# A hybrid layer's input projection, by blocks of full products or by seven products of halves

## The chip, the core and the metric

The kernel runs on one core of a Trainium2 chip. The metric is the time on the device, in microseconds (us), of one launch. Engines are named as in the profile: PE (TensorE, with its weight loads PEld), DVE (VectorE), ACT (ScalarE), POOL (GpSimd) and SP (SyncE, which issues the DMAs here). A matmul result lies in PSUM, in banks of 512 float32 columns.

## The reference

One layer over 2048 tokens of 1024 features, in float32: a norm, one projection to 5120 columns, and two branches that are gated, merged and added to the input.

```python
h = rms_norm(x, norm_gain)
z = h @ w_in                                   # 1024 -> 5120
q, k, v, gate_a, u_s, gate_s, merge_logits = split(z)      # 512 each, the last 2048
q, k = rms_norm of each sub-head of 64, with gains
o_a = diff_attention(q, k, v, ...) * silu(gate_a)          # 4 heads x 2, block-causal
o_s = s5_branch(u_s, ...) * silu(gate_s)                   # diagonal state space, GELU, GLU
g_a, g_s = split(sigmoid(merge_logits + merge_gate_b))
x + (g_a * (o_a @ proj_attn) + g_s * (o_s @ proj_ssm)) @ w_out
```

The change is in the second line, and in when the state space's work is done beside it.

## The kernel before

Everything is held by feature: a tile has 128 features or columns on its partitions and a block of `TB` = 512 tokens along its row. A float32 product is made by `split3` from three matmuls: each operand is cut into an upper half (the cast to the matmul's own float32 type) and a lower half (the rest), and upper × upper, upper × lower and lower × upper are added in one bank. The function `hilo` makes the two halves, the cast on ACT and the difference on DVE or POOL.

`phase1` keeps all of x on chip as two halves, `hh` and `hl`, four blocks of 512 tokens each, not normed; the norm is a factor per token (`E`, later `R`) that is applied to the results. The weights come in 20 groups `g` of 256 columns; groups 0 and 1 are q, 2 and 3 k, 4 and 5 v, 8 and 9 u, the others the gates. Of each tile of 128 columns and each block of tokens, 8 × 3 matmuls of 512 columns fill one bank (`proj`, `proj1`); v is made with the tokens as the stationary operand, 24 matmuls of 256 columns for 128 tokens (`value`). Order: q and v of group 0, then q, v, k, k, u. After each block of q or k comes `qk_norm`: two squares, their sum, the sum over sub-heads on PE (`ms`, lines 231 and 232), a Newton step for the inverse root, and the product's two halves, stored to DRAM as Q or K (four stores of 256 KB).

Behind u stands `mid()`: `ssm_prep` (the state space's matrices for chunks of eight steps, with long complex products on POOL and DVE), `ssm_states` (the scan over chunks), `attn_consts`, and `ssm_out` (16 iterations, each of 12 matmuls of 256 columns into `ps_y`). Then `early()`, which loads K, V and Q of the first head, and the 24 tiles of the gates; the last two tiles (`LATE`) leave their last block of tokens to `last`, called beside the attention. Attention, `glu`, `proj_ssm` and `Tail` follow.

The code is written in this order, but a scheduler in the framework reorders instructions between engines by its own simulated times and fixes one order per engine; each engine then takes its instructions strictly in that order, and waits come only from data and buffers. A pool's tag is a ring of buffers: a new tile waits until the last user of the buffer's old tile, a store's landing included, is through.

Of the kernel before, what the change touches and what calls it, by code (L numbers as in the profile page):

```python
# [21 lines left out]
def f(ap):  # L22
    """The float32 view of a float32r operand."""
    return ap.bitcast(F32)
# [12 lines left out]
LATE = 2  # L37

def split3(nc, out, wh, wl, xh, xl, start, stop):
    """out += w.T x in float32: the three products of the halves that matter at 24 bits."""
    nc.tensor.matmul(out, wh, xh, start=start, stop=False)  # L44
    nc.tensor.matmul(out, wh, xl, start=False, stop=False)  # L45
    nc.tensor.matmul(out, wl, xh, start=False, stop=stop)  # L46
# [43 lines left out]
def newton(nc, k, pool, t, w, out, c=1.0, tags=("n", "n"), bufs=2):  # L90
    """out = c * t ** -0.5 over [128, w]: exp(-ln/2) and one Newton step."""
# [9 lines left out]
def phase1(tc, k, I, mid, early, keep):  # L101
    """The projections of the normed input, and steps that the last of them wait for: the gates' last columns
    over the last tokens."""
    nc = tc.nc
    with ExitStack() as es:
        def pool(name, bufs, e=es, **kw):
            kw = kw or {"side": "right"}
            return e.enter_context(tc.tile_pool(name=name, bufs=bufs, reuse_waits="tile", **kw))

        rp, k.wp = pool("rp", 1, keep), pool("wp", 1, keep)  # L110
        pm = pool("pm", 5, space=PSUM)
        hh, hl = [None] * NTB, [None] * NTB
        for t in reversed(range(NTB)):
            hp = pool(f"hp{t}", 1, keep if t == NTB - 1 else es)
            hh[t] = hp.tile([128, 8, TB], F32R, name=f"hh{t}")
            hl[t] = hp.tile([128, 8, TB], F32R, name=f"hl{t}")
        E = rp.tile([128, T], F32, name="E")
        rc = k.cp.tile([128, 16], F32, name="rc")

        BUFS = {"x": 4, "s": 3, "q": 2, "t": 2, "n": 2, "o": 2, "v": 2}  # L120
        W = {}

        def et(tag, name, dtype=F32):
            return k.ep.tile([128, TB], dtype, tag=tag, name=name, bufs=BUFS[tag])

        def load_w(g, eng=None):
            """Steps that load 256 columns in quarters and split them."""
            W[g] = []
            for i in range(4):
                if i % 2 == 0:  # L130
                    wh = k.wp.tile([128, 4, 256], F32R, tag="wh", bufs=4, name="wh")
                    wl = k.wp.tile([128, 4, 256], F32R, tag="wl", bufs=4, name="wl")
                    W[g].append((wh, wl))
                raw = k.wp.tile([128, 2, 256], F32, tag="wraw", bufs=2, name="wraw")
                o = slice(2 * (i % 2), 2 * (i % 2) + 2)
                nc.sync.dma_start(raw, I["win"][g][:, 2 * i:2 * i + 2])
                if eng:
                    eng.tensor_copy(wh[:, o], raw)  # L138
                else:
                    nc.scalar.copy(wh[:, o], raw)  # L140
                (eng or nc.gpsimd).tensor_tensor(out=wl[:, o], in0=raw, in1=f(wh[:, o]), op=ALU.subtract)  # L141
                yield

        def load_w1(c):
            """One tile of 128 columns in halves, split."""
            wh, wl = (k.wp.tile([128, 8, 128], F32R, tag="wl", bufs=4, name="w1") for _ in range(2))
            for i in range(2):
                raw = k.wp.tile([128, 4, 128], F32, tag="wraw", bufs=2, name="wraw")
                o = slice(4 * i, 4 * i + 4)
                nc.sync.dma_start(raw, I["win"][c // 2][:, o, 128 * (c % 2):128 * (c % 2) + 128])  # L150
                nc.scalar.copy(wh[:, o], raw)
                nc.vector.tensor_tensor(out=wl[:, o], in0=raw, in1=f(wh[:, o]), op=ALU.subtract)
            return wh, wl

        def wk(g, kk, cs):
            return [w[:, kk % 4, cs] for w in W[g][kk // 4]]

        def load_x(t):
            """Steps that load a block of x in halves, and its norms."""
            acc = et("t", "acc")  # L160
            xs = {}
            lag = 2

            def square(kk):
                sq = acc if kk == 0 else et("q", "sq")
                nc.scalar.activation(out=sq, in_=xs[kk], func=AF.Square)
                if kk:
                    nc.gpsimd.tensor_tensor(out=acc, in0=acc, in1=sq, op=ALU.add)

            for kk in range(8):  # L170
                xs[kk] = et("x", "xs")
                nc.sync.dma_start(xs[kk], I["xT"][kk * 128:(kk + 1) * 128, t * TB:(t + 1) * TB])
# [201 lines left out]
NH = 4  # L374
# [836 lines left out]
```

## Time and profile before

| what | value |
|---|---|
| median of three runs | 1813.46 us (1805.32 to 1816.14) |
| span of the profiled execution | 1807.6 us |
| the profiled execution's own time | known by its span alone, 5.9 us below the median |
| mean granted PE clock | 0.979 |
| busy share: PE, PEld, DVE, ACT, POOL | 94%, 79%, 55%, 38%, 18% |
| DMA | 239.06 MB, mean 132 GB/s |

A busy time counts an instruction from start to end; matmuls overlap, so the price of one more is the distance between two starts, which is shorter than its own duration. Rows of the view by lines give, after the bar, the busy sum in us, the mean of one in ns, and the idle time ahead of the group with what ended it. Rows of the view of waits give the engine, tile and line that waited, what it waited for, the sum in us, how often, and the longest. A row of the chain gives the start, the length and the work that the end hung on.

### The profile page before, as it was taken

What the parts mean: (1) busy time and instruction counts of PE and PEld (TensorE: products, weight loads), DVE (VectorE), ACT (ScalarE), POOL (GpSimd) and SP (SyncE); (2) the same over time, 40 slices, a digit from 0 to 9 for tenths busy, and PEclk for the clock granted to TensorE, in tenths of its full rate; (3) what the DMA queues carried; (4) which work ended last, traced back from release to release, by engine and by line L of the source; (5) the groups of instructions that cost most, each with busy time, mean ns of one, the idle gap of its engine ahead of it and who ended that gap; (6) DMA issues with size and microseconds to landing.
All of it is one profiled execution on the core that took longest, in us unless ns stands there. A gap on an engine that the chain in (4) does not pass through costs nothing.

```text
span 1807.6 us, 24838 instructions
## 1 busy us (share of the span) xinstructions
PE 1701.5 (94%) x8720; PEld 1432.4 (79%) x8720; DVE 997.1 (55%) x2400; ACT 682.3 (38%) x1404; POOL 328.1 (18%) x442
## 2 busy tenths in 40 slices
PE   7879798889699999999999999999999999999999
PEld 5777786677588887887888878878888879888887
DVE  7644314469832495495223277678677678643331
ACT  5443222220123413311344366667554567511100
POOL 4331110004200000000345334553011022100000
PEclk9989899999899999999999999999999999999999
DMA  5332322233444323225656584763554543554532
GB/s 168 102 100 87 92 73 72 69 105 84 126 139 121 122 76 122 80 71 158 185 153 169 171 262 116 198 212 112 193 178 133 161 139 117 186 156 151 148 100 82
DMA packets 213005, 239.06 MB, mean 132 GB/s; under 512 B 41456, under 2 KB 151440, under 8 KB 211856
## 3 DMA queue, kind: packets, MB, share of 16 engines
q1 hardware_dynamic: 212880, 237.47, 43.5%
q8 instruction: 69, 1.13, 0.3%
q14 instruction: 56, 0.46, 0.1%
HBM read 146.44 MB, written 90.96 MB: 131 GB/s over the span
## 4 chain that ended last, share of the span: by engine, by line
PE 58%; DMA 17%; DVE 16%; ACT 3%; issue 3%; POOL 1%; SPq 1%; DVEq 0%; ACTq 0%; POOLq 0%
PE ps_p L44 8%; PE ps_p L45 8%; PE ps_p L46 8%; DMA K<-ql 5%; PE ps_o L568 5%; DVE t L879 4%; DMA Q<-ql 4%; PE ps_o L45 3%; PE ps_o L46 3%; PE ps_o L44 3%; PE ps_s L528 3%; PE ps_s L529 3%; PE ps_t L560 2%; DVE V L879 2%; PE ps_a L46 2%
## 5 line engine op out<-in xcount | busy, mean ns | idle before, releaser
L44 PE MATMUL ps_p<-hh,w 128*128 128x512 f32 x896 | 353.6, 395 | 2.4 <-DVE u L313 1.2
L45 PE MATMUL ps_p<-hl,w 128*128 128x512 f32 x896 | 353.2, 394 | 0.0
L46 PE MATMUL ps_p<-hh,w 128*128 128x512 f32 x896 | 352.7, 394 | 0.0
L44 PEld LDWEIGHTS ps_p<-hh,w 128*128 128x128 f32 x896 | 170.5, 190 | 38.0 <-DVE q L240 2.0
L46 PEld LDWEIGHTS ps_p<-hh,w 128*128 128x128 f32 x896 | 170.4, 190 | 35.3 <-issue 0.7
L45 PEld LDWEIGHTS ps_p<-hl,w 128*128 128x128 f32 x896 | 170.4, 190 | 34.5 <-issue 0.7
L541 ACT ACTIVATE e<-e,mm 128x640 f32<-128x640 f32 (+11 forms) x96 | 136.2, 1419 | 63.8 <-DVE mm L539 62.9
L568 PE MATMUL ps_o<-V,at 128*128 128x128 f32 x1088 | 148.5, 276 | 2.3 <-ACT sq L574 1.8
L568 PEld LDWEIGHTS ps_o<-V,at 128*128 128x128 f32 x1088 | 141.4, 192 | 9.3 <-ACT sq L574 2.3
L329 DVE TENSOR_TENSOR z<-ps_p,E 128x512 f32<-128x512 f32 x96 | 65.9, 686 | 132.7 <-PE ps_p L46 132.7
L531 DVE TENSOR_SCALAR_CACHE_REDUCE e<-ps_s 128x512 f32<-128x512 f32 (+1 forms) x192 | 120.6, 640 | 31.2 <-PE ps_s L529 29.7
L528 PE MATMUL ps_s<-K,Q 128*128 128x512 f32 (+3 forms) x320 | 129.0, 405 | 1.1 <-DVE e L531 0.8
L529 PE MATMUL ps_s<-K,Q 128*128 128x512 f32 (+3 forms) x320 | 115.9, 365 | 0.0
L44 PE MATMUL ps_qk<-hh,wh 128*128 128x512 f32 x256 | 101.6, 403 | 12.6 <-DVE wh L138 7.7
L45 PE MATMUL ps_qk<-hl,wh 128*128 128x512 f32 x256 | 101.2, 399 | 1.4 <-DVE hl L175 1.4
L46 PE MATMUL ps_qk<-hh,wl 128*128 128x512 f32 x256 | 101.9, 398 | 0.3 <-DVE wl L141 0.3
L335 ACT ACTIVATE z<-z,hmb 128x512 f32<-128x512 f32 x64 | 46.3, 723 | 144.6 <-DVE z L329 131.0
L560 PE MATMUL ps_t<-ident,e 128*128 128x128 f32 x544 | 85.1, 274 | 4.6 <-ACT at L562 2.5
L551 DVE SCALAR_TENSOR_TENSOR e<-e,cf 128x128 f32<-128x128 f32 (+7 forms) x64 | 88.2, 1378 | 1.4
L562 ACT COPY at<-ps_t 128x512 f32<-128x512 f32 (+3 forms) x160 | 79.3, 522 | 18.4 <-PE ps_t L560 17.8
L560 PEld LDWEIGHTS ps_t<-ident,e 128*128 128x128 f32 x544 | 66.4, 141 | 16.6 <-ACT at L562 4.2
L534 DVE CUSTOM_DVE_ANT_0 e<-ps_s,nb 128x384 f32<-128x384 f32 (+3 forms) x128 | 70.1, 552 | 16.6 <-PE ps_s L529 15.5
(334 smaller groups left out, 3464.4 us busy)
## 6 DMA issues: line engine op xcount, KB each, us to landing
wraw<-win SPq DMA_DIRECT2D x80, 256.0 KB
TM<-z SPq DMA_DIRECT2D x30, 512.0 KB
t<-TM SPq DMA_DIRECT2D x40, 256.0 KB
xs<-xT SPq DMA_DIRECT2D x32, 256.0 KB
u<-US SPq DMA_DIRECT2D x64, 128.0 KB
K<-K SPq DMA_DIRECT2D x8, 1024.0 KB
Q<-Q SPq DMA_DIRECT2D x32, 256.0 KB
Q<-Q SPq DMA_DIRECT2D x64, 128.0 KB
```

Source lines behind the costliest of these rows:

```text
L44: nc.tensor.matmul(out, wh, xh, start=start, stop=False)
L45: nc.tensor.matmul(out, wh, xl, start=False, stop=False)
L46: nc.tensor.matmul(out, wl, xh, start=False, stop=stop)
L528: nc.tensor.matmul(ps, Q[:, 0, s, 128 * b:128 * b + 128], Kt[s][:, ks], start=True, stop=False)
L529: nc.tensor.matmul(ps, Q[:, 1, s, 128 * b:128 * b + 128], Kt[s][:, ks], start=False, stop=True)
L531: nc.vector.tensor_scalar(out=et[:, ks], in0=ps, scalar1=0.0, scalar2=3e38, op0=ALU.add, op1=ALU.min, accum_out=mc[:, i:i + 1])
L541: nc.scalar.activation(out=et, in_=et, func=AF.Exp, bias=mm, scale=-1.0, accum_out=su)
L551: nc.vector.scalar_tensor_tensor(out=e[0], in0=e[1], scalar=cf, in1=e[0], op0=ALU.mult, op1=ALU.add)
L560: nc.tensor.transpose(pt[:, x], e[:, o:o + 128], k.ident)
L562: nc.scalar.copy(AT[g][:, :w], pt[:, :w])
L568: nc.tensor.matmul(po, AT[x // 4][:, x % 4], Vt[x // 8][:, x % 8], start=x == 0, stop=x == n - 1)
L879: tt = lambda o, a, b, op: eng.tensor_tensor(out=o, in0=a, in1=b, op=op)
```

## The change

The projection is done with Strassen's scheme in Winograd's form: features and tokens are cut in two halves each (and the columns of a group in two tiles of 128), and seven products of half size take the place of eight. It runs over one half of 1024 tokens at a time (`sb`), and per half over all 20 groups.

- `first` loads two blocks of tokens, norms them, and makes seven blocks (`BLOCKS`) of 4 × 128 features by 512 tokens: three quarters of the normed x and four sums of quarters. Each is split into halves in a ring of seven buffers, and also stored in DRAM (`BD`).
- `second` does the same for the other two blocks of tokens, in steps between the groups of the first half, into DRAM only. Its norms are products on POOL; x is read twice.
- `turn` loads the other half's seven blocks (28 DMAs of 256 KB) and splits them (ACT and DVE). It is called before the second half, and again between the gates, since the gates run over the second half first.
- `weights` loads four quarters of a group, makes four sums on POOL and splits seven tiles (ACT and DVE). All 20 groups are thus loaded, summed and split twice, once per half.
- `product` is 12 matmuls of 512 columns; `group` makes seven of them, 84 matmuls, with three banks X, Y and Z; ACT copies banks out in the middle of their accumulation, and three of the four results are finished by a sum (two on DVE from PSUM, one on POOL).
- q and k, v, u and the gates are then handled from SBUF. v is turned by four transposes per tile (64 in all) rather than made in its own layout. `qk_norm` takes all its eight tiles from one ring "q" of six; its sum of squares and lower halves of q and k are on POOL.
- The preparation of the state space is a generator, stepped between the groups of the second half, with smaller tiles (complex products of 288 elements a row on POOL, eight by seven, where they had 576). `ssm_out` has a lasting pool `so`, whose tiles `Tail` uses later. `early` comes only after all gates, and nothing is left for beside the attention.

```diff
+BLOCKS = ("11", "21", "T2", "T1", "T3", "22", "T4")
+    def halves(self, n, j, src):
+        nc, b = self.nc, self.B[n]
+        nc.scalar.copy(b[:, 0, j], src)
+        nc.vector.tensor_tensor(out=b[:, 1, j], in0=src, in1=f(b[:, 0, j]), op=ALU.subtract)
+    def norm(self, x, kk, R, eng):
+        gc = self.k.gain[:, kk:kk + 1]
+        if eng is self.nc.vector:
+            eng.scalar_tensor_tensor(out=x, in0=x, scalar=gc, in1=R, op0=ALU.mult, op1=ALU.mult)
+        else:
+            self.nc.scalar.activation(out=x, in_=x, func=AF.Copy, scale=gc)
+            eng.tensor_tensor(out=x, in0=x, in1=R, op=ALU.mult)
+    def combine(self, x11, x12, x21, x22, eng):
+        tt = lambda o, a, b: eng.tensor_tensor(out=o, in0=a, in1=b, op=ALU.subtract)
+        tt(x11, x12, x11)
+        tt(x12, x22, x12)
+        tt(x22, x22, x11)
+        tt(x21, x21, x22)
+        return {"T1": x11, "T3": x12, "T4": x21, "T2": x22}
...
+    def turn(self, sb, tile):
+        for n in BLOCKS:
+            self.slot(n)
+            for j in range(4):
+                x = tile()
+                self.nc.sync.dma_start(x, self.BD[sb][n][j])
+                self.halves(n, j, x)
+    def weights(self, g):
...
+        yield split(a[0, 0])
+        yield split(a[0, 1])
+        s1 = raw()
+        tt(s1, a[1, 0], a[1, 1], ALU.add)
+        tt(a[1, 0], a[0, 0], a[1, 0], ALU.subtract)
+        tt(a[0, 0], s1, a[0, 0], ALU.subtract)
...
+    def product(self, ps, w, n, first):
+        b = self.B[n]
+        for j in range(4):
+            split3(self.nc, ps, w[:, 0, j], w[:, 1, j], b[:, 0, j], b[:, 1, j], first and j == 0, j == 3, not first)
+    def group(self, g, put):
...
+        X = self.bank("ps_x")
+        self.product(X, next(w), "11", True)
+        m1 = copy(X, "m1")
+        Z = self.bank("ps_z")
+        self.product(Z, next(w), "21", True)
+        put(0, 0, Z, m1)
+        self.product(X, next(w), "T2", False)
+        u2 = copy(X, "u2")
+        Y = self.bank("ps_y")
+        self.product(Y, next(w), "T1", True)
+        m5 = copy(Y, "m5")
+        self.product(X, next(w), "T3", False)
+        u3 = copy(X, "u3")
+        put(1, 1, u3, m5)
+        self.product(Y, next(w), "22", False)
+        put(0, 1, Y, u2)
+        self.product(X, next(w), "T4", False)
+        put(1, 0, X, None)
...
+                    for a in range(2):
+                        p.u(8 + a, sb)
+                        step()
+                        p.qk(a, sb, k.qg, k.QT[a])
+                        step()
+                    for a in range(2):
+                        p.v(4 + a, sb)
+                        step()
+                        p.qk(2 + a, sb, k.kg, k.KT[a])
+                        step()
...
+        mid()
+        for g in gates:
+            p.gate(g, 1)
+        p.turn(0, lambda: tr.tile([128, TB], F32, tag="tr", bufs=4, name="x"))
+        for g in gates:
+            p.gate(g, 0)
+    early()
```

First piece: PE at the end of the gates. Before, the attention's first scores (`ps_s`) stand among the matmuls of the gates' last tile (`ps_p`):

```order
L44 MATMUL ps_p<-hh_138,w_8417 128x512
L45 MATMUL ps_p<-hl_139,w_8417 128x512
L46 MATMUL ps_p<-hh_138,w_8418 128x512
L528 MATMUL ps_s<-K,Q 128x128 x2
L528 MATMUL ps_s<-K,Q 128x256
L529 MATMUL ps_s<-K,Q 128x128 x2
L529 MATMUL ps_s<-K,Q 128x256
L44 MATMUL ps_p<-hh_133,w_8322 128x512
```

Now, on the same engine, the last of the gates (`ps_x<-B,w`) is followed by four iterations of the state-space output (rows 642 to 688, twelve matmuls each, of which the first few and the last are shown) before the first scores:

```order
641 L40 MATMUL ps_x<-B,w 128x512 x2
642 L40 MATMUL ps_y<-u,th 128x256
643 L40 MATMUL ps_y<-uh,tm 128x256
644 L40 MATMUL ps_y<-xh,wh 128x256
688 L40 MATMUL ps_y<-xh,w 128x256
689 L653 MATMUL ps_s<-K,Q 128x128 x2
690 L653 MATMUL ps_s<-K,Q 128x256
```

What moved: the output of the state space, which lay wholly under the gates, partly ends behind them, and the first scores come behind it.

Second piece: PE between the two norms of the first group of q in the first half. `ms` is a norm's sum over sub-heads; `ps_x`, `ps_y`, `ps_z` are the banks of the groups that follow:

```order
L386 MATMUL ms<-sh,bones 128x512
L40 MATMUL ps_x<-B,w 128x512 x5
L387 MATMUL ms<-sl,bones 128x512
L40 MATMUL ps_x<-B,w 128x512 x24
L40 MATMUL ps_y<-B,w 128x512 x12
L40 MATMUL ps_z<-B,w 128x512 x10
L40 MATMUL ps_x<-B,w 128x512 x12
L40 MATMUL ps_z<-B,w 128x512 x2
L40 MATMUL ps_x<-B,w 128x512 x12
L386 MATMUL ms<-sh,bones 128x512
```

Before, one `ms` came per block of tokens, a block's 24 × 2 matmuls behind the last; now both norms of a group come due at its end, and their two `ms` stand inside the groups behind it, 77 matmuls apart.

Third piece: POOL in the second half. Before, it had the preparation's complex products (`bigc`, 576 elements) in one run with nothing else between:

```order
L693 TENSOR_TENSOR bigc_3572<-bc,P_3488 128x576
L693 TENSOR_TENSOR bigc_3571<-bc,P_3489 128x576
L693 TENSOR_TENSOR cp_3573<-bigc_3572,bigc_3571 128x576
L693 TENSOR_TENSOR bigc_3571<-bc,P_3488 128x576
L693 TENSOR_TENSOR bigc_3572<-bc,P_3489 128x576
```

Now they (`big`, 288 elements) stand between weight sums (L267), the third result's sum (L323), sums of squares (L382) and lower halves of q and k (L984):

```order
L267 TENSOR_TENSOR raw<-raw 128x512
L984 TENSOR_TENSOR ql<-sq,qh 128x512
L818 TENSOR_TENSOR big_2959<-bC,P_2934 128x288
L818 TENSOR_TENSOR big_2960<-bC,P_2933 128x288
L984 TENSOR_TENSOR ql<-sq,qh 128x512
L267 TENSOR_TENSOR raw<-raw 128x512
L323 TENSOR_TENSOR z<-u_2826,m_2809 128x512
L818 TENSOR_TENSOR cp_3574<-big_2960,big_2959 128x288
L382 TENSOR_TENSOR sq<-sq 128x512
```

What moved: work of the norms, the weights and the state space that lay on other engines or in other stretches shares one queue.

More of the change, by code (lines that the diff above doesn't have):

```diff
@@ L35, with split3 @@
 TAIL = [3, 0, 1, 2]
[L37 to L46, printed above, removed]
+def split3(nc, out, wh, wl, xh, xl, start, stop, more=False):
+    mm = lambda w, x, a, b: nc.tensor.matmul(out, w, x, start=a, stop=b, skip_group_check=more)
+    mm(wh, xh, start, False)
+    mm(wh, xl, False, False)
+    mm(wl, xh, False, stop)
 def consts(tc, k, I):
@@ L104, in phase1 @@
+def phase1(tc, k, I, prep, mid, early):
     nc = tc.nc
     with ExitStack() as es:
[L106 to L153, printed above, removed]
@@ L340, in phase1 @@
-        cols = (12, 13, 14, 15, 20, 21, 22, 23, *range(24, 40))
-        n = len(cols) - LATE
-        for c in cols[:n]:
-            gate(c, range(NTB))
-        w = {c: gate(c, range(NTB - 1)) for c in cols[n:]}
-    def last(ps):
-        for c in (*cols[-2:], *cols[n:-2]):
-            gate(c, (NTB - 1,), w[c] if c in cols[-2:] else None, ps)
-    return last
+        p = Proj(tc, k, I, es)
+        gates = (6, 7, 10, 11, *range(12, 20))
+        with ExitStack() as e1:
+            p.pn = p.pool("pn", e1, space=PSUM)
+            nc.sync.dma_start(k.ident, I["ident"])
+            with ExitStack() as e0:
+                p.ep, p.ex, p.nx = p.pool("ep0", e0), p.pool("ex0", e0), 16
+                p.first()
+            p.ep = p.pool("ep", e1)
+            for sb in range(2):
+                with ExitStack() as e2:
+                    if sb == 0:
+                        p.ex, p.nx = p.pool("ex", e2), 5
+                        it = p.second()
+                    else:
+                        it = prep()
+                    step = lambda: next(it, None)
+                    for a in range(2):
[8 more added lines that the diff above has]
+                        step()
+                    for _ in it:
+                        pass
+                    if sb == 0:
+                        p.turn(1, p.x)
@@ L756, in ssm_prep @@
         bb = [t(f"bb{i}", [128, 16, 16]) for i in range(2)]
-        big = [t(f"big{i}", [128, 4 * 144]) for i in range(2)]
+        big = [t(f"big{i}", [128, 288]) for i in range(2)]
+        yield
         b16 = [b[:, :256].rearrange("p (a b) -> p a b", b=16) for b in big]
@@ new lines, in ssm_matrices @@
+        for q in range(0, 16, 2):
+            out = [p.tile([128, 2, 8, 16], F32, tag=f"cp{i}", name=f"wn{i}") for i in range(2)]
+            s = slice(q, q + 2)
+            cmul(v, out[0], out[1], cc[0][:, s], cc[1][:, s], pj[0][:, s, 0:8], pj[1][:, s, 0:8], w[0], w[1])
+            ps = k.pF.tile([128, 2, 2, 2, 64], F32, tag="F", bufs=k.NF, name="ps_w")
+            for y in range(2):
+                for r in range(2):
+                    nc.tensor.transpose(ps[:, y, r].rearrange("p x q -> p (x q)"),
+                                        out[r][:, y].rearrange("p j h -> p (j h)"), k.ident)
+            wi = p.tile([128, 2, 2, 2, 64], F32, tag="wi", name="wi")
+            for y in range(2):
+                nc.scalar.copy(wi[:, y].rearrange("p x r q -> p r x q"), ps[:, y])
+            nc.sync.dma_start(k.WD[:, 2 * q:2 * q + 4], wi.rearrange("p y x r q -> p (y x) (r q)"))
+            if q == 6:
+                yield
@@ L817, in ssm_prep @@
+    yield
     with ExitStack() as e2:
-        with tc.tile_pool(name="sp4", bufs=1, side="right", reuse_waits="tile") as p2:
+        with tc.tile_pool(name="sp4", bufs=1, reuse_waits="tile") as p2:
             dd = p2.tile([16, 32], F32, name="dd")
```

569 lines of the change are left out of this document (307 added, 262 removed).

## The prediction

> **What bounds the kernel now.** I read the head of the page first, for the engine that is busy and the clock, and then a table of busy time by stage: up to 46 us the start, to 495 us q, k, v, u and the preparation of the state space, to 1046 us the gates with the scan and the state-space output beside them, then the attention and the rest.
>
> ```profile
> span 1807.6 us, 24838 instructions
> PE 1701.5 (94%) x8720; PEld 1432.4 (79%) x8720; DVE 997.1 (55%) x2400; ACT 682.3 (38%) x1404; POOL 328.1 (18%) x442
> ```
> ```profile
> 0.00:46.00 46.00, 33.33 (x170) 27.01 (x171) 32.95 (x53) 25.48 (x45) 19.52 (x25) 1.00 0.57 170
> 46.00:495.00 449.00, 381.43 (x1888) 322.19 (x1887) 234.49 (x543) 122.09 (x225) 81.99 (x63) 0.93 0.32 91
> 495.00:1046.00 551.00, 545.59 (x2552) 453.16 (x2551) 259.43 (x595) 178.22 (x343) 77.05 (x87) 0.99 0.44 133
> 1046.00:1808.00 762.00, 741.16 (x4114) 630.03 (x4112) 470.19 (x1211) 356.49 (x792) 149.52 (x268) 1.00 0.50 154
> ```
>
> The columns are start and end, length, busy us of PE, its weight loads, VectorE, ScalarE and GpSimd, the granted clock, the DMA share and GB/s. PE is busy 545.59 of 551 us in the gates: fewer matmuls there are time saved. From 46 to 495 us it idles for 67.6 us (449 − 381.4) and its 381 us ran at 0.93 of the clock, another 381.4 × 0.07 = 27 us. What it waits for there stands in the waits and in the chain that ended last:
>
> ```profile
> PE ms L231 <- ACT sh L842: 39.0, 9, 11.0
> DVE ql L844 <- DMA Q<-ql: 64.5, 9, 9.5
> DVE ql L844 <- DMA K<-ql: 60.6, 12, 7.7
> ```
> ```profile
> 146.32 8.69 DMA Q<-ql
> ```
>
> The norms of q and k wait for their stores to land (8.69 us in this link), and PE waits for the norms. So one half of the projection is bound by PE, the other by side work.
>
> **The change: what PE saves.** Matmuls are pipelined, so their price is the step from start to start:
>
> ```profile
> 1029.69 0.39 PE L46 MATMUL ps_p<-hh,w 128*128 128x512 f32 x1
> ...
> 1046.01 0.40 PE L46 MATMUL ps_p<-hh,w 128*128 128x512 f32 x1
> 1046.24 0.50 PE L528 MATMUL ps_s<-K,Q 128*128 128x128 f32 x3
> ```
> ```profile
> 26.11 0.28 PE L252 MATMUL ps_v<-wh,hh 128*128 128x256 f32 x1
> ...
> 27.05 0.28 PE L253 MATMUL ps_v<-wl,hh 128*128 128x256 f32 x1
> ```
> ```profile
> 1181.40 1.79 PE ps_o L568 x16
> ```
>
> From the first to the third row lie 73 matmuls, so 512 columns cost 16.32/72 = 0.2267 us up to the last of them; 256 columns cost 0.94/8 = 0.1175, 128 columns 1.79/16 = 0.112. Before, the projection has 3456 matmuls of 512 columns (q and k 768, u 384, gates 2304) and 768 of 256 for v: 783.5 + 90.2 = 873.7 us. After, it has 20 groups × 2 halves × 84 = 3360 of 512 and 64 transposes: 761.7 + 7.2 = 768.9. PE saves **105 us**; a group costs 84 × 0.2267 = 19.04 us. The 48 matmuls left beside the attention (48 × 0.2267 = 10.9 us) go from there.
>
> **What the side engines gain.** The seven products are paid for in sums and splits on VectorE, GpSimd and ScalarE. How two of these share the memory shows at 46 us:
>
> ```profile
> 45.96 2.99 POOL L168 TENSOR_TENSOR acc<-acc,sq 128x512 f32<-128x512 f32 x2 [0.44 <-ACT sq L166]
> ...
> 45.99 1.81 DVE L96 TENSOR_TENSOR nw_a<-nw_y,tt 128x512 f32<-128x512 f32 x1
> ...
> 47.73 1.77 DVE L175 SCALAR_TENSOR_TENSOR hl<-xs,small,hh 128x512 fp32r<-128x512 f32 x1
> ...
> 49.42 0.68 DVE L97 SCALAR_TENSOR_TENSOR nw_a<-nw_a,nw_y 128x512 f32<-128x512 f32 x1
> ```
> ```profile
> 427.55 1.43 POOL L693 TENSOR_TENSOR cp<-bigc,bigc 128x576 f32<-128x576 f32 x1
> ...
> 427.64 1.37 DVE L693 TENSOR_TENSOR L<-big,big 128x16 f32<-128x16 f32 x1
> ```
> ```profile
> 902.76 0.69 DVE L946 TENSOR_TENSOR z<-ps_y,y 128x512 f32<-128x512 f32 x1 [0.26 <-POOL y L945]
> 902.81 1.30 POOL L844 TENSOR_TENSOR x<-x,xh 128x512 fp32r<-128x512 f32 x1
> ```
>
> A VectorE instruction with two inputs from SBUF takes 0.68 us alone and 1.81 or 1.77 beside a GpSimd one; even 16 elements a row last 1.37. One with an input from PSUM isn't held (0.69 beside 1.30). So the two engines take turns, and a pair costs about 1.79 us (the mean of 1.81 and 1.77); I split it as 0.57 for VectorE and 1.22 for GpSimd, estimates that leave out the latency at an instruction's start.
>
> The Trainium skill, page "SBUF — State Buffer", section "SBUF: two separate sides", says that GpSimd and a VectorE instruction with two SBUF inputs hold a shared pair of ports in turn for a whole instruction, and names no PSUM input among the blocked. The trace agrees (1.81 against 0.68; 0.69 beside 1.30). Had the two sums per group that read PSUM to wait too, as they don't by that rule, 40 groups would add 2 × 0.69 × 40 = 55 us to what follows.
>
> Counted from the code, VectorE with two SBUF inputs and GpSimd, both of 512 elements a row:
> - Start, first half and turn: 62 on VectorE for `first` (12 norms, 16 combinations, 28 splits, 6 in the inverse), 56 weight splits, 48 in eight norms, 24 in `second`, 28 in `turn`: 218 × 0.57 = 124 us. GpSimd: 4 + 32 weight sums + 8 + 24 in the norms + 30 in `second` = 98 × 1.22 = 120 us. From 12 us on (an estimate for the first loads and squares), taking turns ends at **256 us**.
> - Second half's eight groups and three gate groups: 125 × 0.57 = 71, 79 × 1.22 = 96. The preparation: 56 GpSimd instructions of 288 elements, about 0.7 us each by half of the row of 576 below, 39; VectorE some 40 (an estimate: a bit under half of the 83 us that it was busy in the two rows below). Sum 246, so 19 groups are done at **502 us**.
>
> ```profile
> L693 POOL TENSOR_TENSOR bigc<-bc,P 128x576 f32<-128x576 f32 x16 | 19.7, 1251 | 168.2 <-DVE P L693 167.7
> L168 POOL TENSOR_TENSOR acc<-acc,sq 128x512 f32<-128x512 f32 x28 | 39.3, 1404 | 62.6 <-ACT sq L166 61.6
> L152 DVE TENSOR_TENSOR w<-wraw,w 128x512 fp32r<-128x512 f32 x56 | 38.7, 714 | 0.1
> L151 ACT CAST w<-wraw 128x512 fp32r<-128x512 f32 x56 | 32.1, 618 | 93.4 <-PE ps_p L45 62.2 <-DMA wraw<-win 31.0
> ```
> ```profile
> 405.00:450.00 45.00, 44.73 (x198) 36.72 (x196) 43.48 (x147) 2.29 (x4) 20.67 (x18) 1.00 0.37 90
> 450.00:495.00 45.00, 30.09 (x120) 24.11 (x121) 39.49 (x164) 6.91 (x14) 13.47 (x11) 0.89 0.44 127
> ```
>
> PE alone would have them at 40 + 19 × 19.04 + 20 for norms and transposes = 422 us. Between 422 and 502 lies the main unknown; I take 502, since the trace shows the turn-taking wherever both engines have work.
>
> The other 21 groups are gates: 21 × 19.04 = 400 us of PE against 7 × 0.57 + 5 × 1.22 + 2 × 0.69 = 11.5 us a group on the side, so PE sets the pace, as from 495 to 1046 us. Added: 30 us of the state space's own matmuls (ps_k 64 × 0.112, the states 96 × 0.1175, half of ps_y 96 × 0.1175), and 25 where the scan's VectorE work or the second `turn` (28 splits at 0.714 = 20 us, ScalarE 28 × 0.618 = 17, in a group of 19) exceeds PE's. 502 + 455 = 957. Then four iterations of the state-space output stand alone on PE (the first piece in the section on the change): per iteration GpSimd alone has 4.7 us (tm, u, w, x and y at 0.74, 1.3, 0.74, 1.3 and 0.62), so 19 to 40, I take 26: the attention starts at **983** against 1046. That is a gain of 63.
>
> From there 762 − 10.9 (the late matmuls) + 5.6 (four iterations' 48 × 0.1175) + 12 = 769 us; the 12 are for K, V and Q of the first head, loaded only now, where before they lay under gates (an estimate between nothing and two landings of 8.69). The span is 983 + 769 = 1752, with 10 for waits in order that no sum holds **1762**. The profiled execution's time is known by its span of 1807.6, 5.9 below the median of the three runs, 1813.46; the same step gives 1768, and I say **1765**.
>
> Extra transfers: the first 256 us move about 51 MB (x 12.6, blocks stored 14.7 and loaded 7.3, weights 8.4, results 8.4), 200 GB/s, where 170 GB/s took a share of 0.57 (first row of the stages). At 0.67 this costs nothing by itself, unless landings grow.
>
> **The rivals.**
> - *The buffers hide the side work* and PE is paced by itself: 19 groups at 422 to 450 us, so 1690 to 1715. For it: half of GpSimd's work in the first half (`second`) may run late into the second. Against: the sums are of whole stages, and no buffer hides a mean. Chance 0.2.
> - *Copies in mid-accumulation come late.* Bank X is copied by ScalarE between its products, with 12 matmuls = 2.72 us to do so (one other product lies between). ScalarE has some 15 of 19 us of work per group in program order, splits of 0.618 us and norms among it. A copy late by 0.3 us, 160 times: 48 us, 1813, no change. Chance 0.12.
> - *Each wait costs clock too.* From 46 to 495 us the clock was 0.93 with 15% idle; 19.04/0.93 = 20.5 us is still under the 25 us a group that the turns take, so I cost it at nothing. If the waits come in one piece per group and PE then is at half pace over a critical stretch of about 1.7 us, 19 groups give 32 us: 1797. Chance 0.08. The Trainium skill, page "TensorE: Matmul & The Clock Gate", Part 1, has such a fall to half after an idle window of about 3.4 us; by it the loss per wait is an estimated 1.7 us, while the trace shows only the means.
> - *Stores set the pace, slower than before.* Place: `qk_norm`, ring "q" of six tiles with eight used per norm; the second norm of each q or k group can't have its sh before the first norm's qh has landed. Between the two `ms` PE has 77 matmuls (the second piece in the section on the change), 17.5 us; the chain between takes some 8.5 us (an estimate) and a landing. Up to a landing of 9 us it fits (8.69 above), beyond it PE stands for the rest, in eight groups. The gain of 48 is gone from a landing of 15 us; at 20, eight times 11, 88 us: 1853. For it: before, this was the chain's longest run of links. Against: those 17.5 us. Chance 0.17.
>
> **How the numbers follow.** My forecast, turn-taking to 502 us, has 0.43: 1735 to 1795. A measurement here tells about 1% from no change: faster is below 1795, slower above 1831. Faster: 0.43 + 0.2 and half of the clock's rival, 0.67; same: 0.12 + 0.04 and 0.02 of the stores' rival, its mild end, 0.18; slower: the rest of it, 0.15. The range leaves out most of the stores' rival and the tip of the first: **1690 to 1835**.
>
> **What would show it.** VectorE's splits (`w<-raw`) and combinations with means over 1.2 us and GpSimd busy over half of the first 500 us; PE idle by 70 to 100 us there, over 98% busy in the gates; the first ps_s of the attention near 983 us. If PE is busy throughout before 500 us, the first rival holds; waits of the banks for `copy` show the second; PE's `ms` waiting over 5 us eight times, with landings over 12, the fourth. I am wrong most likely in how far the turns overlap with PE across groups.

## The result, and the profile after

The changed kernel takes 1962.13 us (median; 1958.98 to 1967.9), the kernel before 1810.43 beside it: a ratio of **1.0849** (95% interval 1.0814 to 1.0884), slower by 152 us where a gain of 48 was forecast, and far outside the range. The head of the page and the table by stage, cut at the points that the prediction speaks of (columns as before):

```profile
span 1966.1 us, 24659 instructions
## 1 busy us (share of the span) xinstructions
PE 1683.8 (86%) x7948; PEld 1365.0 (69%) x7948; DVE 1253.2 (64%) x2438; ACT 917.0 (47%) x1816; POOL 701.2 (36%) x704
```
```profile
0.00:80.00 80.00, 42.50 (x115) 25.79 (x116) 61.20 (x83) 41.88 (x73) 23.30 (x26) 0.79 0.56 193
80.00:322.00 242.00, 164.82 (x641) 126.41 (x639) 130.05 (x137) 101.92 (x179) 125.66 (x85) 0.84 0.43 133
322.00:651.00 329.00, 261.80 (x1039) 199.51 (x1039) 219.56 (x380) 144.43 (x257) 171.74 (x139) 0.87 0.45 133
651.00:1165.00 514.00, 461.99 (x1998) 371.98 (x1997) 361.66 (x615) 252.75 (x474) 191.90 (x151) 0.94 0.44 143
1196.00:1966.00 770.00, 741.18 (x4112) 632.04 (x4112) 475.91 (x1218) 365.24 (x814) 173.22 (x288) 0.99 0.51 156
```

No engine is near its limit in the first three rows: PE idles in the projection, and DVE and POOL do too: up to 651 us at least one of the two is busy for 516 us, and for 135 us both stand. In the gates, where PE was busy 545.59 of 551 us, it now idles for 52 of 514. The starts of every 84th product matmul in the trace give the groups' times (group 0 is the first; in each half u and q alternate twice, then v and k, and from group 16 on all are gates):

| point | forecast, us | measured, us |
|---|---|---|
| group 8 begins (first half and turn done) | 256 | 322.6 |
| group 19 begins | 502 | 651.0 |
| last matmul of the gates | 957 | 1165.0 |
| first scores of the attention | 983 | 1196.1 |
| from there to the end | 769 | 770 |

Cutting each step from one matmul's start to the next into its price (0.2267 us per 512 columns), a gap (what is over, where it is more than 1.3 prices) and slow pace (the rest) gives PE's account up to the first scores: before, 908 us of price, 92 of gaps, 38 of slow pace; after, 815, **296** and 79. The change saved 93 us of matmuls and paid 204 in gaps and 41 in slow pace, 245 together.

### The profile page after: what moved, and what is told of

It reads as the page before. It is cut to its first block, busy times and chain, and to the rows that moved or that the text cites. A ratio compares the mean times of both kernels' runs of the same rounds, so it can differ in the third digit from the quotient of the medians.

```text
span 1966.1 us, 24659 instructions
## 1 busy us (share of the span) xinstructions
PE 1683.8 (86%) x7948; PEld 1365.0 (69%) x7948; DVE 1253.2 (64%) x2438; ACT 917.0 (47%) x1816; POOL 701.2 (36%) x704
## 4 chain that ended last, share of the span: by engine, by line
PE 33%; DVE 13%; DMA 13%; issue 5%; ACT 4%; POOL 3%; SPq 1%; POOLq 0%; ACTq 0%; DVEq 0%
PE ps_o L40 8%; PE ps_x L40 5%; DVE t L1019 4%; PE ps_a L40 3%; PE ps_p L40 3%; PE ps_o L693 3%; PE ps_y L40 3%; DVE w L264 2%; DVE V L1019 2%; PE ps_s L654 1%; PE ps_s L653 1%; PE ps_z L40 1%; PE ps_t L685 1%; DMA XD<-V 1%; DMA raw<-proj_attn 1%
## 5 line engine op out<-in xcount | busy, mean ns | idle before, releaser
L40 PE MATMUL ps_x<-B,w 128*128 128x512 f32 x1920 | 515.3, 419 | 109.4 <-ACT B L144 51.0
L40 PEld LDWEIGHTS ps_x<-B,w 128*128 128x128 f32 x1920 | 383.2, 203 | 213.8 <-ACT B L144 54.9
L267 POOL TENSOR_TENSOR raw<-raw 128x512 f32<-128x512 f32 x160 | 236.7, 1479 | 421.7 <-DMA raw<-win 209.8
L264 DVE TENSOR_TENSOR w<-raw,w 128x512 fp32r<-128x512 f32 x280 | 252.9, 908 | 164.8 <-ACT w L263 156.4
L40 PE MATMUL ps_y<-B,w 128*128 128x512 f32 x960 | 258.6, 412 | 24.3 <-ACT B L144 7.3
L40 PEld LDWEIGHTS ps_y<-B,w 128*128 128x128 f32 x960 | 188.8, 199 | 73.1 <-ACT B L144 9.0
L263 ACT CAST w<-raw 128x512 fp32r<-128x512 f32 x280 | 171.4, 622 | 81.4 <-POOL raw L267 41.2
L40 PE MATMUL ps_z<-B,w 128*128 128x512 f32 x480 | 123.5, 398 | 4.5 <-ACT B L144 4.5
L40 PEld LDWEIGHTS ps_z<-B,w 128*128 128x128 f32 x480 | 91.0, 192 | 24.7 <-ACT B L144 5.4
L40 PE MATMUL ps_o<-mm,wo 128*128 128x512 f32 x390 | 96.7, 394 | 0.1
```

The costliest lines, as they stand in the source:

```text
L40: mm = lambda w, x, a, b: nc.tensor.matmul(out, w, x, start=a, stop=b, skip_group_check=more)
L263: nc.scalar.copy(w[:, 0], src)
L264: nc.vector.tensor_tensor(out=w[:, 1], in0=src, in1=f(w[:, 0]), op=ALU.subtract)
L267: tt = lambda o, x, y, op: nc.gpsimd.tensor_tensor(out=o, in0=x, in1=y, op=op)
```

## The experiments

Ratios are against the kernel before, measured beside each version; "gain" is against the 1962 us of the changed kernel, "scores" the start of the attention (1196 in it). Differences of some 6 us tell nothing: prep_apart, whose engines work in the order of the changed kernel, differs from it by as much.

### The turns of DVE and POOL

Rows of the groups, the changed kernel first, then the one with all elementwise work of the projection on DVE:

```profile
L267 POOL TENSOR_TENSOR raw<-raw 128x512 f32<-128x512 f32 x160 | 236.7, 1479 | 421.7 <-DMA raw<-win 209.8 <-DVE w L264 81.9 <-issue 23.9
L264 DVE TENSOR_TENSOR w<-raw,w 128x512 fp32r<-128x512 f32 x280 | 252.9, 908 | 164.8 <-ACT w L263 156.4 <-POOL big L818 5.8 <-PE ps_y L40 1.2
```
```profile
L264 DVE TENSOR_TENSOR w<-raw,w 128x512 fp32r<-128x512 f32 x280 | 194.9, 701 | 45.3 <-ACT w L263 43.0 <-PE ps_v L40 2.0 <-issue 0.2
L267 DVE TENSOR_TENSOR raw<-raw 128x512 f32<-128x512 f32 x160 | 112.7, 705 | 62.2 <-DMA raw<-win 60.2 <-DVE w L264 0.9
```

A split took 0.908 us in the mean of all 280, against 0.701: the turns are there, at a fifth of what a full turn at every split would cost. In the changed kernel's trace 127 of the splits overlap an instruction of POOL and take 1.18 us in the mean, up to 1.81; the other 153 take 0.685. Half of POOL's idle time ahead of the sums (209.8 of 421.7 us) ends with the weights' load.

**weights_dve**, the four weight sums on DVE:

```diff
-        tt = lambda o, x, y, op: nc.gpsimd.tensor_tensor(out=o, in0=x, in1=y, op=op)
+        tt = lambda o, x, y, op: nc.vector.tensor_tensor(out=o, in0=x, in1=y, op=op)
```


> The four sums of each group's weights (160 in all) move from POOL to DVE; nothing is left out. Theory of turns (DVE with two SBUF inputs and POOL hold the memory in turn, and the amount of their work sets the first 19 groups): each sum costs 0.57 instead of 1.22 us, 50 us in the first 19 groups and little in the gates, about 1910 us. Theory of the late weight (PE waits for a link of the way from a weight's load over its sum and its split to the matmul, whatever the amount of work): four sums in a row get 3 us shorter, in the gates too, some 2 us in each of 40 groups, about 1880 us.

1919.98 us (1.0586, 1.053 to 1.0642), gain 42, scores at 1129.9: less than either theory, and nearer to the turns' 1910 than to the late weight's 1880.

**no_wsums**, no sums, and **sums_aside**, the same four sums into a scratch tile (both `raw` with `bufs=5`). Of sums_aside the first sum is shown; no_wsums has `s1 = a[1, 1]` and none of the four:

```diff
-        s1 = raw()
-        tt(s1, a[1, 0], a[1, 1], ALU.add)
+        s1, scr = a[1, 1], wp.tile([128, 4, 128], F32, tag="scr", bufs=1, name="scr")
+        tt(scr, a[1, 0], a[1, 1], ALU.add)
...
```


> The four sums of each group's weights are left out (three of the seven products use a plain quarter), the ring of loaded quarters is five tiles for four in use. Turns: 160 x 1.22 us of POOL's work gone, 93 us of it in the first 19 groups, little in the gates: about 1870 us. Late weight: a load goes straight to its split, so the gates come to 19 to 21 us a group instead of 25 and the first groups lose some 4 us each: about 1780 us.

> POOL makes the same four sums of each group's weights, from the same tiles, but into a scratch tile that nobody reads; the products use plain quarters as in the kernel without the sums, with the same ring. POOL's work, and its turns with DVE, stay; that the splits wait for the sums is gone. Turns: as the changed kernel, about 1960 us. Late weight: within 30 us of the kernel without the sums, below 1830 us.

1899.73 us (1.0474, 1.0426 to 1.0523) and 1977.94 us (1.0906, 1.0858 to 1.0954). With the sums made but needed by nobody nothing is gained; without them 62 us are. So it is not that the splits wait for the sums; POOL's work itself costs. Whether by its turns or by holding the loaded quarters, these two runs do not separate. The late weight falls in this form.

**all_dve**, norms, third sums, squares and lower halves on DVE as well (`nc.gpsimd` to `nc.vector` at L164, L218, L323, L382 and the `ql` of `qk_norm`):

> All of the projection's elementwise work on POOL (weight sums, third sums, sums of squares, norms, lower halves of q and k) moves to DVE; POOL keeps the state space's. Nothing is left out. Turns: 177 instructions in the first 19 groups cost 0.57 instead of 1.22 us, 115 us less, and 40 to 50 us less in the rest: about 1810 us. Late weight: as with the weight sums on DVE or a little more, 1850 to 1880 us, since DVE's queue gets longer ahead of every split.

1913.37 us (1.055, 1.0508 to 1.0591), scores at 1108.4: POOL is idle from 80 us to the end of the first half, so there are no turns, and 49 us are gained, not 150. Groups 1 to 6 still take 25.9 us in the mean (28.0 in the changed kernel). Taking POOL's work away thus recovers a third of the loss. It is not a clean price of the turns, since DVE does that work instead.

**no_wsums6**, as no_wsums with `bufs=6`:

> As the kernel without weight sums (1900 us), but the ring of loaded quarters has six tiles instead of five for four in use. Theory of the loop (a quarter's load waits for a buffer that the group before frees by its late splits, holding the DMA queue of SP, so loads, sums, splits and matmuls chase each other round with little slack): one tile more starts loads a split earlier, 40 us less, about 1860 us. Rival (the ring has slack, other values are late): 1890 us or more.

1908.49 us (1.0518, 1.0416 to 1.062): one buffer more gains nothing.

### The turn of the halves

PE at the end of the first half, with the wait ahead of each row in brackets:

```profile
289.50 1.11 PE L354 MATMUL ps_v<-ident,vt 128*128 128x128 f32 x4 [9.16 <-ACT v L356]
295.28 1.12 PE L354 MATMUL ps_v<-ident,vt 128*128 128x128 f32 x4 [4.67 <-ACT v L356]
305.17 0.80 PE L386 MATMUL ms<-sh,bones 128*128 128x512 f32 x1 [8.77 <-ACT sh L982]
...
322.64 0.79 PE L40 MATMUL ps_x<-B,w 128*128 128x512 f32 x1 [15.47 <-ACT B L144]
```

Four stops in a row make a stretch of 42.5 us between two product matmuls. Only the last of them ends with a block of the turn; the others end with copies of v and a norm's `sh` on ACT. On POOL a norm of `second` stood for its x, whose ring of five tiles waits for the stores of `BD`. On ACT the copies and squares stood for stores of K that still held tiles of ring q, and the first block's cast stands directly behind such a square:

```profile
314.03 1.26 POOL L164 TENSOR_TENSOR x<-x,R 128x512 f32<-128x512 f32 x1 [9.57 <-DMA x<-xT]
```
```profile
294.64 0.58 ACT L356 COPY v<-ps_v 128x512 f32<-128x512 f32 x1 [5.20 <-DMA K<-qh]
321.34 0.63 ACT L381 ACTIVATE sq<-z 128x512 f32<-128x512 f32 x1 [2.18 <-DMA K<-qh]
321.97 0.62 ACT L144 CAST B<-x 128x512 fp32r<-128x512 f32 x1
```

**second_out**:

```diff
-                        it = p.second()
+                        it = iter(())
...
-                self.nc.sync.dma_start(x, self.BD[sb][n][j])
+                o = (BLOCKS.index(n) + j) % 8
+                self.nc.sync.dma_start(x, self.I["xT"][128 * o:128 * o + 128, 1024:1536] if sb else self.BD[sb][n][j])
```


> The changed kernel without the second half's squares, norms and sums (`second` is left out); the turn loads 28 tiles of x as they are, so its transfers and splits stay. Theory of late links (PE stops for single values that come late, each stop with a few us of half clock behind it): at the first turn PE stood for 42.5 us and group 8 took 50.6 us, since the blocks are loaded only when the last steps of `second` have stored them; without them a turn costs 10 to 15 us as the second one did, and 30 POOL instructions go, so about 1860 us. Rival, the turn is bound by its own loads and splits: the 42.5 us stay at 30 or more, about 1930 us.

1882.54 us (1.0416, 1.0372 to 1.046), gain **80**, the largest from leaving out one part of the projection. Groups 7 and 8 take 25.5 and 32.7 us instead of 74.6 and 50.6, which is 67 of the 80. The turn's own loads and splits, still made, cost little: the two groups are about as long as their neighbours (33.0 and 22.7).

**all_dve_early**, all_dve with two steps of `second` between groups:

```diff
-                    step = lambda: next(it, None)
+                    step = (lambda: (next(it, None), next(it, None))) if sb == 0 else (lambda: next(it, None))
```


> All elementwise work of the projection on DVE, and `second` steps twice between groups, so that it is through after four of the eight groups; nothing is left out. Against 1913 us with the work on DVE alone. Late links: the blocks lie in DRAM when the turn begins, which saves some 50 us there, and the first four groups lose some 15: about 1875 us. Rival (the turn is bound by its loads and splits): 1910 us or more.

1885.18 us (1.0431, 1.0393 to 1.0468), with nothing left out: 28 us less than all_dve; group 7 falls from 66.8 to 30.7 us, groups 9 to 13 get slower.

### Copies, norms, stores, queues

**no_copy** (`copy` returns a constant tile, for which the ring m has three tiles instead of four) and **no_norm** (z is copied and stored; a group's two norms are gone):

```diff
-            s = self.m(name)
-            nc.scalar.copy(s, ps)
-            return s
+            return self.junk
```


> The changed kernel without the 160 copies of banks that ScalarE makes in the middle of their accumulation; the sums read a constant tile in their place, all other work stays. Rival of the late copies: PE stood 24 us for them by the waits (u 19.0, m 4.9 into ps_x), each with half clock behind, and ScalarE has 94 us less in its queue: about 1900 us. If they are covered: 1950 us or more.

> The changed kernel without the norms of q and k: the projection's z is copied by ScalarE and stored four times, without squares, sums over sub-heads on PE, inverse root and halves. The rival of the stores and the ring has PE stand for `ms`: 26.9 us by the waits, and DVE loses 112 and POOL 48 instructions. Late links: 16 norms, each with a stop of about 2 us and the half clock behind it, and turns of 112 x 0.57 + 48 x 1.22 = 122 us of which PE's waits were a part: about 1860 us. If the norms are covered: 1940 us.

1944.55 us (1.0759, 1.0711 to 1.0807) and 1941.68 us (1.0743, 1.0705 to 1.0781), gains of 18 and 20. In both, PE stands for something else instead. From 80 to 650 us of the changed kernel it waits 26.9 us in 8 waits for the norms' `sh` and 16.0 us in 7 for the copy `u`; in the same stretch, without the copies (first row) the one grows, without the norms (second row) the other:

```profile
PE ms L386 <- ACT sh L982: 55.9, 14, 10.4
```
```profile
PE ps_x L40 <- ACT u L294: 76.0, 7, 18.5
```

So neither gain is the price of the part left out. Without the norms, groups 1 to 6 take 28.3 us in the mean as before, but unevenly, from 19.0 to 42.2. The order on SP has changed with them: z is stored as soon as it is copied, so up to eight stores of Q or K follow each other, where the changed kernel has at most four (how such a burst stops PE stands under bare). What the norms cost stays open.

**pool_queue**, all_dve_early with the weights' loads issued from POOL:

```diff
-            nc.sync.dma_start(a[i, j], self.I["win"][g][:, i, 4 * j:4 * j + 4])
+            nc.gpsimd.dma_start(a[i, j], self.I["win"][g][:, i, 4 * j:4 * j + 4])
```


> As the kernel with all elementwise work on DVE and an early `second` (1885 us), but the loads of the weights are issued from POOL, which is nearly idle there; SP's queue has no wait for weight buffers any more (312.8 us in 92 waits in the changed kernel). Theory of the loop through SP: stores and x come in time and the groups lose some 3 us each: about 1800 us. Rival (SP's waits cost nothing): 1880 us; in the second half POOL's own work behind waiting loads can make it slower still, 1900 us.

1891.92 us (1.0427, 1.0345 to 1.0509): not faster than from SP. The theory that SP's 312.8 us of waits for weight buffers set the pace falls, at least for the first half, where POOL has hardly any other work and group 8 begins at 263.6 us (265.9 in all_dve_early).

**free_rings** and **free_all** (the latter on all_dve_early), stores from a fixed tile, with `self.fixed(1)` in place of `f(qh)`, `f(ql)` and `v`, `self.fixed(2)` in place of u:

> The changed kernel, but the stores of Q, K, V and u read a fixed tile instead of the ring's tile (wrong values are stored, with the same bytes and counts), so that no tile of the rings q and z waits for a store to land. Theory of the stores (the chain from 120 to 230 us goes through landings of 6 to 11 us, which hold a tile; ACT, DVE or POOL then stops in order in front of it, and copies and splits behind it come late): groups 2 to 6 and 9 to 15 come from 28 us to 23, 60 us less in sum, about 1900 us. Rival (the landings lie beside other waits of the same length): 1950 us or more.

> As the kernel with the elementwise work on DVE and an early `second` (1885 us), with the stores of Q, K, V and u from a fixed tile. Theory of the stores: with the turns gone too, groups 2 to 6 and 9 to 15 come to 21 us, 80 us less, about 1805 us. Rival (DVE's own work is the bound there): 26 us a group, 1870 us or more.

1993.15 us (1.098, 1.0923 to 1.1038) and 1915.81 us (1.0554, 1.0498 to 1.0611), slower than with the rings' tiles. Freed from the values, the stores moved ahead of the loads of weights and x (group 2 takes 62.2 us in free_rings, and PE waits for ACT's splits). They tell nothing of the landings, and all_off, which has them, tells less than it was made for.

**ring9**, second_out with nine tiles in the first half's ring q:

```diff
-            p.ep = p.pool("ep", e1)
+                    p.ep, p.nq = p.pool(f"ep{sb + 1}", e2), 6 if sb else 9
```


> As the kernel without `second` (1883 us), with nine tiles instead of six in the ring q of the first half (the second half has six, in a pool of its own). It replaces the fixed tile, which let stores run ahead of loads. Theory of the stores: norms, v and halves no longer wait for landings of 6 to 9 us, groups 2 to 6 of the first half come from 26 us to 21 or 22. Rival: they stay at 25 to 27 us. The total falls by 20 us at most, since one half alone is changed.

Groups 2 to 6 take 114.2 us together, 22.8 each, against 130.8 in second_out: three tiles more in the ring gain 3 us a group there, as the theory of the stores says. The changed kernel itself has the path of that theory, in its second group of q. The square of the second norm waits on ACT for a store of the first norm's half to land, and POOL's sum, ACT's `sh` and PE follow:

```profile
196.19 0.63 ACT L381 ACTIVATE sq<-z 128x512 f32<-128x512 f32 x1 [4.13 <-DMA Q<-qh]
```
```profile
196.96 1.26 POOL L382 TENSOR_TENSOR sq<-sq 128x512 f32<-128x512 f32 x1 [3.87 <-ACT sq L381]
```
```profile
198.92 0.79 PE L386 MATMUL ms<-sh,bones 128*128 128x512 f32 x1 [4.32 <-ACT sh L982]
```

In all ring9 takes 1899.35 us (1.0487, 1.0457 to 1.0518) against 1882.54: the scores begin 13 us earlier, at 1106.3, and what follows takes 792 us instead of 763.

**own_rings**, all_dve_early with the norms' scratch in other rings and four tiles in ring q (two of its changes):

```diff
-        sq = [self.q("sq") for _ in range(2)]
+        sq = [self.q("sq", F32, "s", 2) for _ in range(2)]
...
-            hilo(nc, qh, q, ql, nc.vector)
+            hilo(nc, qh, q, None, nc.vector)
```


> As the kernel with the elementwise work on DVE and an early `second` (1885 us), nothing left out: the norms' squares have a ring of two and their halves use the ring of the inverse root, so that only the four tiles that are stored, in a ring of four, wait for landings, at DVE's last step of a norm and not at its first. Theory of the stores: half of what the fixed tile brings, about 1845 us. Rival: 1875 us or more.

1872.22 us (1.0314, 1.0241 to 1.0387), the fastest version that computes everything: a gain of 90, still 3% behind the kernel before. Its scores begin at 1056, 10 us later than before the change, but 13 of the 16 iterations of the state-space output now follow them (4 in the changed kernel), and the rest takes 819 us instead of 770.

**bare**, second_out and no_norm at once:

> The changed kernel without `second` and without the norms of q and k at once (each as it was left out alone: x loaded as it is at the turn, z copied and stored). Theory of full queues (no single link holds the first groups; weight work alone runs at 19 us a group, as the gates without the state space do, and every other work put into the same in-order queues stops PE now and then): groups 1 to 6 come to 19 to 21 us where leaving out one of the two left 25 and 28, and 9 to 15, with the preparation still there, to 23: about 1830 us. Rival (the groups' own copies, splits and puts need more than 19 us there): 25 us a group still, 1870 us.

1877.03 us (1.0364, 1.0334 to 1.0394), the rival's total, but with the theory's groups: 1, 2, 4 and 6 run at 19.0 to 19.5 us, so their own copies, splits and sums keep pace. Groups 3, 5 and 7 take 32.5 to 34.4, each with one stop. Each stands two groups behind a group of q or k, whose stores it meets. For group 3, SP, POOL, ACT and PE (SP's rows are its issues; L385 and L386 are the stores of Q, L260 the loads of weights; four rows are left out):

```profile
98.30 0.33 SPq L260 DMA_DIRECT2D raw<-win  x1
102.09 0.65 SPq L385 DMA_DIRECT2D Q<-q  x1
102.80 0.55 SPq L386 DMA_DIRECT2D Q<-q  x1
...
108.60 4.45 SPq L385 DMA_DIRECT2D Q<-q  x1
113.10 2.50 SPq L386 DMA_DIRECT2D Q<-q  x1
115.70 3.77 SPq L260 DMA_DIRECT2D raw<-win  x3
```
```profile
128.17 5.28 POOL L268 TENSOR_TENSOR raw<-raw 128x512 f32<-128x512 f32 x4 [30.48 <-DMA raw<-win]
```
```profile
132.14 0.62 ACT L264 CAST w<-raw 128x512 fp32r<-128x512 f32 x1 [18.50 <-POOL raw L268]
132.66 0.58 ACT L295 COPY u<-ps_x 128x512 f32<-128x512 f32 x1
```
```profile
117.30 2.88 PE L40 MATMUL ps_y<-B,w 128*128 128x512 f32 x12
...
133.30 5.32 PE L40 MATMUL ps_x<-B,w 128*128 128x512 f32 x12 [10.85 <-ACT u L295]
```

Both blocks' stores, eight of 256 KB, come due together. Their issue alone takes 13.5 us; the next loads of weights stand behind them in SP's order, and the one that POOL's sums wait for lands 10 us after its issue (the chain has `raw<-win` at 9.79). POOL's sums follow at 128, ACT's split at 132.14, and only behind that split, in ACT's order, the copy of bank X for which PE stands. The twelve matmuls behind the stop take 5.32 us, where twelve took 2.88 before it.

Each link is in the trace, but the burst is this version's own. With the norms left out nothing spreads the stores; the changed kernel has at most four of them in a row, at a median issue of 0.53 us. So bare shows how a stop runs through ordered queues, and that the first half's groups reach 19 us without `second` and the norms; it does not show that such bursts cost the changed kernel its time.

### The state space

**prep_apart** (all of `ssm_prep` called in `mid`, nothing between the groups):

> The changed kernel with the preparation of the state space in one piece behind the second half's groups, ahead of the scan, rather than stepped between those groups; nothing is left out. If the interleaving makes the second half slow (groups 9 to 15 of 27 us), these come to 22 us, 35 us less, and the preparation's DVE work falls into the first gates, which costs as much again: 1940 to 1970 us. If PE waits there for other things: 1960 us or more, with groups 9 to 15 unchanged at 26 us.

1967.97 us (1.0846, 1.0775 to 1.0917). The scheduler gave all four compute engines the very order of instructions that they have in the changed kernel, and groups 9 to 15 are as they were to within 0.2 us. So nothing was taken apart: the 6 us between the totals are the spread between measurements, and what interleaving costs stays open.

**no_ssm** (neither `ssm_states` nor `ssm_out`):

> The changed kernel without the scan and the state space's output (`ssm_states`, `ssm_out`; zeros are stored in their place): their 30 to 40 us of matmuls go, and DVE's, ACT's and POOL's work for them. In the gates PE stood 84 us in gaps and lost 31 at low clock. If the gates are slow because their splits and copies queue behind that work: gate groups of 19.1 to 20 us from the fourth on, attention some 150 us earlier, about 1810 us. If the gates' own way of weights makes the gaps: 22 us a group still, about 1880 us.

1857.57 us (1.0238, 1.0177 to 1.0299), gain **105**, of which the left-out matmuls are 34 (96 + 192 at 0.1175). Its gates, and two gate groups of the changed kernel beside the scan:

```profile
680.00:1072.00 392.00, 386.60 (x1688) 316.88 (x1686) 169.35 (x214) 185.37 (x307) 134.75 (x98) 1.00 0.41 139
```
```profile
743.00:797.00 54.00, 45.48 (x178) 36.52 (x177) 52.76 (x100) 19.57 (x34) 13.68 (x10) 0.87 0.31 96
```
```profile
PE ps_x L40 <- DVE w L264: 8.5, 2, 4.7
```
```profile
782.17 0.58 DVE L1019 TENSOR_TENSOR t<-V,L 128x256 f32<-128x256 f32 x1
782.67 1.56 DVE L1019 TENSOR_TENSOR t<-V,LS 128x256 f32<-128x256 f32 x1
784.16 1.71 DVE L264 TENSOR_TENSOR w<-raw,w 128x512 fp32r<-128x512 f32 x1
```

Alone, 15 of the 18 groups from 21 to 38 run at 19.0 us with the same weights, copies, splits and stores (three by the second turn at 19.7 to 23.5): the scheme itself keeps PE full. Beside the scan DVE is full (52.76 of 54 us), splits stand behind scan steps (L1019 in the last rows, where sums run on POOL and the last step and the split take longer too), and two of them stop PE for 8.5 us. The account of these 53.6 us has 38.8 of price, 9.6 of gaps, and 5.2 of slow pace behind them: the clock was 0.87.

**all_off** (free_all without the state space):

> The kernel with the work on DVE, an early `second` and stores from a fixed tile, without the scan and the state space's output as well. If the causes found (turns, the late blocks at the turn, landings, the state space's work in the gates) are all there is: groups of 19 to 21 us throughout, start of the attention near 950 us and 1720 us in all. If something else holds the first 16 groups: these stay at 26 us, 1800 us.

1823.24 us (1.0072, 1.0052 to 1.0092): still not under the kernel before; gates at 19.0, but groups 1 to 15 at their uneven pace, stores ahead of loads included.

## Why the prediction was wrong

- **PE's saving** was right: 105 us by the sum, 93 by the account up to the scores, the 10.9 us of late matmuls not in it. So were the 19.04 us of an undisturbed group (19.0 in no_ssm). The stretch behind the first scores came out as forecast, 769 against 770, in part by luck: in the other versions it took 762 to 819.
- **The step that failed** is the one from volumes to time: "taking turns ends at 256 us" and "19 groups are done at 502 us", with "10 for waits in order that no sum holds". I added up the work of DVE and POOL, took the sum as the stages' time, and put all waits at 10 us. The volume was about right: 490 us of turns up to group 19, against 516 in which at least one of the two was busy (with some work in it that I had not counted). The time was not: both stood idle for 135 us beside that, and PE's gaps up to the scores are 296.
- **The turns** are real and were over-weighted. A split took 0.908 us in the mean, not the 1.79 of a pair, and moving POOL's work or leaving its sums out gained 42 to 62 us, where the sum let the turns add 80 to PE's 422. The signs that I named did not come: split means over 1.2 us, POOL busy over half of the first 500 us (244), PE idle for 70 to 100 us there (150) and over 98% busy in the gates (90%).
- **The first turn** was costed at 16 us of splits. Groups 7 and 8 around it took 125 us, and 58 without `second`, whose loads, norms and stores share the queues with the last norms of k and their stores.
- **The gates** were to be paced by PE "as from 495 to 1046 us", with 25 us for the scan and the turn: 84 of gaps and 31 of slow pace were measured from 651 us to the scores (with the 31 us behind the last gate, where 26 were forecast). Before, a split of weights served 48 matmuls, and a bank's 24 needed one product on DVE, in a ring of five banks; now each 12 matmuls need a fresh split from the engine that runs the scan. My sum compared totals per group, 11.5 us against 19, and left out when each split has to come.
- **The rivals** of the stores, the copies and the clock each name a path that the traces have. The first two were far from the size that they needed. PE waited for `ms` 26.9 us in 8 waits, at landings of 6 to 9 us, where that rival was priced at 88 us and landings of 20. For the copies it waited 24 us, and leaving them out gained 18, where 48 were priced. That these paths act together fits no_copy and no_norm, where PE stands for another value instead, but no run shows it for the changed kernel. The clock's rival was priced at 32 and came near: slow pace rose by 41, from 38 to 79. No run shows its 1.7 us per wait: in group 24, behind a gap of 4.8 us, twelve steps from one matmul to the next take 0.427 us instead of 0.227, and the group's slow pace is 2.5 us. By the rule of the Trainium skill, page "TensorE: Matmul & The Clock Gate", Part 1, an idle window of about 3.4 us halves the clock, and the trace agrees with such a fall.

What remains open: what norms and stores cost in the first half, what the preparation costs in the second, and the first group, which waits for the blocks of `first` and takes 48 to 56 us in every version. No version brought the mean of groups 1 to 15 under 26 us.

## What to carry to other kernels

A scheme that trades matmuls for sums and splits also trades away slack: ask for each matmul what must have been made fresh for it, by which engine's order, and what else stands in that order. Sums of busy time per stage give a floor, not a time; where no engine is busy throughout, the time is in the links, and the price of each is to be read from the waits with the slow clock behind it. Do first the work that a later turn waits for. And before you read an experiment's time, look at the engines' orders: leaving work out can bring a stop of its own, as the burst of stores in bare, and an edit of the code can leave every order as it was, as in prep_apart.

## What the hardware showed beyond that

The issue of a store of 256 KB on SP, 0.52 us in the median for Q in the kernel before, took up to 4.45 us when eight followed each other in bare. The DMA engines were busy for 0.23 of the time on average meanwhile, and for 0.41 in the 12 us behind, in which the load behind the stores was under way; it landed 10 us after its issue, where the same loads, issued from POOL, take 4.4 in the median in pool_queue:

```profile
102.00:116.00 14.00, 14.00 (x64) 11.59 (x63) 4.46 (x7) 6.58 (x13) 0.00 (x0) 1.00 0.23 80
116.00:128.00 12.00, 6.44 (x29) 5.01 (x27) 0.00 (x0) 0.00 (x0) 0.00 (x0) 0.86 0.41 147
```

So here issues and a load were slow while the engines' mean share was under half. What held them, the trace does not show.
